# Two-layer mixer and FFN block: attention's stacks on GpSimd's queue, out-projection weights split once, Strassen sums in place

## The chip, the cores and the metric

One core of a Trainium2 chip runs the whole kernel in one launch. The metric is device time in microseconds of an execution. TensorE is the matmul engine (PE), VectorE is DVE, ScalarE is ACT, GpSimd is POOL, SyncE is SP; each has a queue of its own that it works off in order, and a DMA is issued by an instruction in one of these queues.

## What is computed

Two layers over 1024 latent tokens and 256 context tokens, 1024 features, all in float32. Cut to what the change touches (`hc` is the context):

```python
for l in range(DEPTH):                                       # 2
    u_lat = modulate(rms_norm(h, norm1_g[l]), sh1, sc1)
    y_lat, y_ctx = hybrid_mixer(u_lat, u_ctx, ...)           # mLSTM, attention, pool, conv: 256 columns each
    h = h + g1 * (y_lat @ w_out[l])                          # out-projection, 1024 x 1024
    h = h + g2 * swiglu(modulate(rms_norm(h, norm2_g[l]), sh2, sc2), ffn_w_in[l], ffn_w_out[l])
    if l == 0:
        hc = hc + cg1 * (y_ctx @ w_out[l])
        hc = hc + cg2 * swiglu(modulate(rms_norm(hc, ...), ...), ...)

# attention, 4 heads, two softmaxes per head over 1280 keys
s = jnp.einsum('bqhmd,bkhmd->bhmqk', q, k) * (A_HD ** -0.5)  # m = 0, 1; d = 32
p = jax.nn.softmax(s, axis=-1)
o = jnp.einsum('bhqk,bkhe->bqhe', p[:, :, 0] - lam * p[:, :, 1], v)
```

## The kernel before, in words

Activations lie with features on the partitions, eight tiles of 128 features, and tokens along the columns. A float32 product is made of three matmuls on rounded parts: `hi` is a rounded copy (ACT) and `lo` the rest (DVE or POOL subtracts), and `mm3` adds hi x hi, lo x hi and hi x lo. `load_w` (its load is L304, the subtraction L297) loads a raw 128 x 512 weight tile into one of two buffers and splits it into one of five pairs. Calls to the engines pass through a wrapper, so that most instructions have line 165; there tiles tell them apart. The program's text is the order in each engine's queue, apart from what its generators interleave (below); every DMA is issued on SP's queue.

A layer goes through these stages. **Mixers**: projections of the four mixers; `qk_in` makes normalised, rotated q and k, splits them and stores hi and lo to a DRAM scratch (`qks`). **Attention**: `stacks(h)` loads head h's operands from that scratch into 128 partitions. For each m it fills 128 rows of `Qs` with two loads (hi twice, lo twice) and of `Ks` with one (hi and lo, twice), so one plain matmul of 128 rows does the whole product. `dup` makes this source pattern, with an outermost step of 0 that reads everything twice. Head h + 1 is loaded from the third slot of head h. `attention` places its steps in numbered slots of one score group each: scores, maximum (DVE `ls`), exponential (ACT `pr`), the combination of the two softmaxes (POOL and DVE in turn, `combine`), transposes (`atp`), and the product with V (`po`).

**Out-projection**: `out_early` brings in the first six y tiles and four weight tiles during the last head. `out_proj` walks over blocks of tokens (512, 512 and 256 context columns in layer 0; 512, 256 and 256 in layer 1). In each block it loads h, and for each of eight feature tiles `nt` it takes two weight tiles (`out_w`), does 24 matmuls into `ops`, adds the scaled result into h (DVE `h<-ops`), stores h to `hmid`, and advances `later` by three steps. `later` holds the steps of `norm_ffn`'s `chunk` for the blocks done before: squares (ACT `nsq`), their sum over features (PE `nps`), the reciprocal root (DVE), scaling (DVE `h<-h,Af,nrstd`, ACT adds the bias), then the sums of the FFN's Strassen scheme (POOL and DVE into temporary tiles `t`), each split into `Uh` (ACT) and `Ul` (DVE). **FFN**: `ffn_in` loads its weights as `fr`, splits them into `fh` and `fl` (DVE), multiplies into `fps`; then `ffn_out`.

Of the kernel before, what the change touches and what calls it, by code (L numbers as in the profile page):

```python
# [184 lines left out]
class Builder:  # L185
# [299 lines left out]
    def norm_r(self, h, c0, n):  # L485

        nc = self.nc
# [9 lines left out]
        sm = self.T("nsum")[:, :n]  # L497
        self.copy(sm, px[:, :n])
        px = self.PX("nps2")
        nc.tensor.matmul(px[:, :n], self.cb("comb", P), sm, start=True, stop=True)  # L500
        r = self.T("nrstd")[:, :n]
        self.rsqrt(r, px[:, :n], 1e-6, sm)
        return r
# [447 lines left out]
    def qk_in(self, kind, i, c0, n, ps):  # L951
# [24 lines left out]
        for x, v in enumerate((hi, lo)):  # L976
            nc.sync.dma_start(self.qk_scr[kind, 4 * i:4 * i + 4, x, :, c0:c0 + n].bitcast(F32), v.bitcast(F32))
# [179 lines left out]
    def attention(self, early):  # L1157
# [4 lines left out]
        gd = nc.sync.dma_start  # L1162
# [194 lines left out]
    def load_y(self, hi, lo, k, cs):  # L1357

        self.nc.sync.dma_start(lo.bitcast(F32), self.y_scr[k][:, cs])
        self.copy(hi, lo.bitcast(F32))  # L1360
        self.sub_lo(lo, lo.bitcast(F32), hi)

    def first_y(self, k, c0, n):
        t = self.U(f"y{k}", F32R)
        hi, lo = t[:, 0:n], t[:, 512:512 + n]
        self.load_y(hi, lo, k, slice(c0, c0 + n))
        self.y0[k] = (hi, lo)

    def out_w(self, l, nt, pc):
        return self.load_w(self.a["w_out"][l, nt, pc], 512, self.nc.gpsimd, "wo")  # L1370

    def out_early(self, l, chunk):

        self.y0, self.w0 = {}, []
        for i, k in enumerate(self.YORDER[:6]):
            self.first_y(k, *chunk)
            yield
            if i < 4:
                self.w0.append(self.out_w(l, i // 2, i % 2))
                yield  # L1380

    def out_proj(self, l, src, dst, chunks, later):
# [5 lines left out]
        for i, (c0, n) in enumerate(chunks):  # L1388
            v = 1 if c0 < NCTX else 0
            cs = slice(c0, c0 + n)  # L1390
            if i == 0:
                for k in order[6:]:
                    self.first_y(k, c0, n)
                y = self.y0
            else:
                y = {}
                for k in order:
                    y[k] = self.E("yh", KT, F32R)[:, :n], self.E("yl", KT, F32R)[:, :n]
                    self.load_y(*y[k], k, cs)
# [22 lines left out]
    def norm_ffn(self, l, need):  # L1422
# [9 lines left out]
        def chunk(h, c0, n):  # L1432
# [13 lines left out]
            a, b = slice(0, m), slice(m, n)  # L1446
            blk = lambda x: x.rearrange("p (s j) -> p s j", j=P)
            for k in range(4):
                for x in (k, k + 4):
                    hv = h[x][:, :n]  # L1450
                    nc.vector.scalar_tensor_tensor(hv, hv, A[:, x, v:v + 1], r, ALU.mult, ALU.mult)
                    nc.scalar.activation(hv, hv, AF.Identity, bias=B(x))
                yield
# [353 lines left out]
```

## Time and profile before

| What | Value |
|---|---|
| Median of 3 runs | 3509.52 us (3508.51 to 3517.68) |
| Profiled execution | 3513.39 us |
| Its span, first to last instruction | 3511.6 us |
| Mean granted TensorE clock | 0.93 |
| PE busy | 3038.5 us (87%) |
| DVE, ACT, POOL busy | 1950.9, 1356.1, 875.4 us |
| DMA | 368.05 MB, mean 105 GB/s, SP's queue 33.0% of 16 engines |

An engine counts as busy while an instruction of its own runs; DMA issues do not count. "PEclk" or clock is the share of TensorE's full clock that was granted, and a wait is put down to the releaser that came last. Layer 0's attention starts near 554 us and its out-projection lies around 850 to 1012; layer 1's are near 2395 and 2670 to 2816.

### The profile page before, as it was taken

The numbers are of one execution on the slowest core, as the hardware profiler recorded it, in microseconds if no ns is written. First come the engines' busy times: TensorE is split into PE (matmuls) and PEld (weight loads), VectorE is DVE, ScalarE is ACT, GpSimd is POOL, SyncE is SP. The second block draws the span as 40 slices with busy tenths as digits, with TensorE's granted clock in tenths as the row PEclk, the third lists the DMA queues.
The fourth block names the chain that finished last, engine by engine and source line by source line (L and its number), as shares of the span: only waits on it lengthen the run. The fifth ranks groups of instructions, "written<-read, shape, count | busy, mean of one in ns | idle before, by whom it ended". The sixth has DMA issues, their size and how long they took to land. (4 is left out here: it accounts for less than half of the span.)

```text
span 3511.6 us, 44759 instructions
## 1 busy us (share of the span) xinstructions
PE 3038.5 (87%) x16354; PEld 2432.8 (69%) x16354; DVE 1950.9 (56%) x3022; ACT 1356.1 (39%) x2664; POOL 875.4 (25%) x634
## 2 busy tenths in 40 slices
PE   7999883778878999999998898873778779999999
PEld 3757662556667888888886777562557568888787
DVE  5593553874456666663336377543773654544343
ACT  4213442765443222223335422433774543333232
POOL 2241210212533333230001132210232543442000
PEclk9999986898989999999999999986899889999999
DMA  7123221113523443444444311221114422322644
GB/s 264 52 80 98 86 83 57 65 61 107 155 80 108 120 121 99 123 123 155 154 146 156 109 45 43 87 82 56 64 62 128 128 88 81 86 83 60 198 162 138
DMA packets 251246, 368.05 MB, mean 105 GB/s; under 512 B 32401, under 2 KB 109841, under 8 KB 251025
## 3 DMA queue, kind: packets, MB, share of 16 engines
q1 hardware_dynamic: 251024, 365.19, 33.0%
q8 instruction: 129, 2.11, 0.3%
q14 instruction: 93, 0.75, 0.1%
HBM read 295.89 MB, written 69.21 MB: 104 GB/s over the span
## 5 line engine op out<-in xcount | busy, mean ns | idle before, releaser
L165 PE MATMUL fps<-Uh,fh 128*128 128x512 f32 (+1 forms) x1288 | 496.3, 386 | 38.9 <-ACT fh L165 26.1
L165 PE MATMUL fps<-Ul,fh 128*128 128x512 f32 (+1 forms) x1288 | 494.5, 384 | 0.0
L165 PE MATMUL fps<-Uh,fl 128*128 128x512 f32 (+1 forms) x1288 | 493.8, 384 | 0.6 <-DVE fl L165 0.6
L165 ACT ACTIVATE fh<-fr 128x512 fp32r<-128x512 f32 x330 | 207.0, 631 | 529.7 <-PE fps L165 391.0
L165 DVE TENSOR_TENSOR fl<-fr,fh 128x512 fp32r<-128x512 f32 x330 | 270.9, 822 | 133.4 <-ACT fh L165 132.6
L165 PE MATMUL xps<-gl,xh 128*128 128x512 f32 (+1 forms) x880 | 327.3, 373 | 12.8 <-DVE gl L165 12.7
L165 PE MATMUL xps<-gh,xh 128*128 128x512 f32 (+1 forms) x880 | 327.7, 373 | 9.8 <-ACT xh L165 7.5
L165 PE MATMUL xps<-gh,xl 128*128 128x512 f32 (+1 forms) x880 | 326.2, 372 | 0.2 <-DVE xl L165 0.2
L165 PEld LDWEIGHTS fps<-Uh,fh 128*128 128x128 f32 x1288 | 245.6, 191 | 91.5 <-ACT fh L165 28.6
L165 PE MATMUL sc<-Ks,Qs 128*128 128x512 f32 (+1 forms) x400 | 130.5, 437 | 186.6 <-DMA Ks<-qks 108.6
L165 DVE TENSOR_TENSOR ft<-fps,ft 128x512 f32<-128x512 f32 (+1 forms) x230 | 152.7, 664 | 234.9 <-PE fps L165 230.6
L165 PEld LDWEIGHTS fps<-Uh,fl 128*128 128x128 f32 x1288 | 245.2, 190 | 50.3 <-DVE fl L165 1.7
L165 PEld LDWEIGHTS fps<-Ul,fh 128*128 128x128 f32 x1288 | 245.9, 191 | 43.7 <-issue 0.8
L165 DVE TENSOR_REDUCE ls<-sc 128x1 f32<-128x1280 f32 (+1 forms) x144 | 195.4, 1367 | 130.0 <-PE sc L165 129.7
L165 PE MATMUL fmps<-uh,wfh 128*128 128x512 f32 (+1 forms) x592 | 223.8, 378 | 14.9 <-ACT kT L165 14.9
L165 PEld LDWEIGHTS sc<-Ks,Qs 128*128 128x128 f32 x400 | 76.1, 218 | 220.4 <-issue 107.0
L165 ACT ACTIVATE pr<-sc,ls 128x1280 f32<-128x1280 f32 (+1 forms) x144 | 178.4, 1239 | 129.4 <-DVE ls L165 126.1
L165 PE MATMUL fmps<-uh,wfl 128*128 128x512 f32 (+1 forms) x592 | 224.0, 378 | 0.0
L165 PE MATMUL fmps<-ul,wfh 128*128 128x512 f32 (+1 forms) x592 | 223.3, 377 | 0.0
L165 DVE TENSOR_TENSOR gl<-gl,gh 128x512 fp32r<-128x512 f32 (+1 forms) x110 | 70.9, 644 | 264.4 <-ACT gh L165 264.1
L1223 POOL TENSOR_TENSOR pr<-pr,pr 128x1280 f32<-128x1280 f32 (+1 forms) x36 | 95.9, 2663 | 422.7 <-DVE pr L165 225.0
L165 DVE SCALAR_TENSOR_TENSOR acc<-cy,par,acc 128x1286 f32<-128x1286 f32 (+28 forms) x120 | 199.4, 1699 | 1.0
(304 smaller groups left out, 6620.5 us busy)
## 6 DMA issues: line engine op xcount, KB each, us to landing
xr<-in_ffn_out SPq DMA_DIRECT2D x220, 256.0 KB
fr<-in_ffn_in SPq DMA_DIRECT2D x176, 256.0 KB
mw<-in_mod_w SPq DMA_DIRECT2D x160, 256.0 KB
gs<-ft SPq DMA_DIRECT2D x99, 256.0 KB
wor<-in_w_out SPq DMA_DIRECT2D x96, 256.0 KB
gl<-gs SPq DMA_DIRECT2D x88, 256.0 KB
wfr<-in_w_fm SPq DMA_DIRECT2D x56, 256.0 KB
Ks<-qks SPq DMA_DIRECT2D x16, 640.0 KB
```

Source lines behind the costliest of these rows:

```text
L165: ins = f(*args, **kw)
L1223: nc.gpsimd.tensor_tensor(pr[0][:, :n], pr[0][:, :n], pr[1][:, :n], ALU.add)
```

## The change

- The 44 stores of `qk_in` and the 48 loads of Q and K stacks (32 and 16) are issued on POOL's queue; the loads of V stay on SP's.
- `out_w` splits each of the 16 out-projection weight tiles in a layer's first block only, and stores hi and lo to a DRAM scratch (`wos`, 256 KB each); later blocks load hi and lo from there. In counts over both layers: raw loads 96 before and 32 now, `wos` stores 64, `wos` loads 96.
- In layer 1 the blocks are 512 and 512, as in the FFN, not 512, 256 and 256.
- The squares of the norm are summed inside the out-projection, one `nt` behind the result (`norm_sums`, `norm_fin`); the context block's are not formed there.
- The Strassen sums overwrite h's tiles, in the order in which the FFN uses them (B11, B22, T2, T3, T1, B21, T4). Per 512 columns DVE does 8 scalings, 20 splits and 12 differences of 256 columns, POOL 4 differences and 8 splits; the temporaries are gone.
- `out_early` first issues the six y loads, with each split three steps behind, and then the four weight tiles.

```diff
+    def norm_sums(self, n):
         px = self.PX("nps")
         for k in range(KT):
+            v = yield
             sq = self.T("nsq")
-            v = h[k][:, c0:c0 + n]
-            nc.scalar.activation(sq[:, :n], v, AF.Square)
+            self.nc.scalar.activation(sq[:, :n], v[:, :n], AF.Square)
             g = slice((k % 4) * 32, (k % 4) * 32 + 32)
-            nc.tensor.matmul(px[g, :n], self.cb("one", 32), sq[:, :n], start=(k < 4), stop=(k >= 4))
+            self.nc.tensor.matmul(px[g, :n], self.cb("one", 32), sq[:, :n], start=(k < 4), stop=(k >= 4))
...
-            nc.sync.dma_start(self.qk_scr[kind, 4 * i:4 * i + 4, x, :, c0:c0 + n].bitcast(F32), v.bitcast(F32))
+            nc.gpsimd.dma_start(self.qk_scr[kind, 4 * i:4 * i + 4, x, :, c0:c0 + n].bitcast(F32), v.bitcast(F32))
...
-        gd = nc.sync.dma_start
+        gd = nc.gpsimd.dma_start
...
+    def out_w(self, l, nt, pc, first):
+
+        if first:
+            w = self.load_w(self.a["w_out"][l, nt, pc], 512, self.nc.gpsimd, "wo")
+            for x in range(2):
+                self.nc.sync.dma_start(self.wo_scr[nt, pc, x], w[x][:, :512].bitcast(F32))
+            return w
+        w = [self.wp.tile([P, 544], F32R, tag=t, name=t, bufs=5) for t in ("wh", "wl")]
+        for x in range(2):
+            self.nc.sync.dma_start(w[x][:, :512].bitcast(F32), self.wo_scr[nt, pc, x])
+        return w
...
+        for i in range(len(ks) + 3):
+            if i < len(ks):
+                self.load_y(ks[i], *chunk, True)
+            if i >= 3:
+                self.split_y(ks[i - 3])
             yield
-            if i < 4:
-                self.w0.append(self.out_w(l, i // 2, i % 2))
-                yield
+        for i in range(4):
+            self.w0.append(self.out_w(l, i // 2, i % 2, True))
+            yield
...
+            squares = self.norm_sum(n) if not v else None
...
-                w = [self.w0.pop(0) if self.w0 else self.out_w(l, nt, pc) for pc in range(2)]
+                w = [self.w0.pop(0) if self.w0 else self.out_w(l, nt, pc, i == 0) for pc in range(2)]
...
+                if squares and nt:
+                    squares.send(h[nt - 1])
             if i == 0:
                 self.ux.close()
-            todo = itertools.chain(todo, later(h, c0, n))
+            if squares:
+                squares.send(h[KT - 1])
+                todo = itertools.chain(todo, later(h, c0, n))
...
-            if v:
-                return
-            r = yield from self.norm_r(h, 0, n)
-            B = lambda k: mod[:, 24 + k, v:v + 1]
...
+            for k in (0, 4, 1, 5, 2, 6, 3, 7):
+                hv = h[k][:, :n]
+                nc.vector.scalar_tensor_tensor(hv, hv, A[:, k, v:v + 1], r, ALU.mult, ALU.mult)
+                nc.scalar.activation(hv, hv, AF.Identity, bias=mod[:, 24 + k, v:v + 1])
+                if k >= 4:
+                    yield
...
+            def split(i, src, eng):
+                for k in range(4):
+                    hi, lo = (x[:, i, cs].rearrange("p (s j) -> p s j", j=P) for x in state["U"][k])
+                    self.copy(hi, half(*src(k)))
+                    eng(lo, half(*src(k)), hi.bitcast(F32), ALU.subtract)
+                    if k % 2:
+                        yield
+            def minus(a, b, eng):
+                for k in range(4):
+                    eng(half(*b(k)), half(*a(k)), half(*b(k)), ALU.subtract)
+            u1a, u1b, u2a, u2b = ((lambda k, x=x, i=i: (h[k + x], i)) for x in (0, 4) for i in range(2))
+            yield from split(self.B11, u1a, d)
+            minus(u1b, u1a, g)
+            minus(u2b, u1b, d)
+            yield from split(self.B22, u2b, g)
             for k in range(4):
+                d(half(*u2b(k)), half(*u2b(k)), half(*u1a(k)), ALU.subtract)
+            yield from split(self.T2, u2b, d)
+            yield from split(self.T3, u1b, d)
+            yield from split(self.T1, u1a, g)
+            yield from split(self.B21, u2a, d)
+            for k in range(4):
+                d(half(*u2a(k)), half(*u2a(k)), half(*u2b(k)), ALU.subtract)
+            yield from split(self.T4, u2a, d)
...
-            oc = LATE if need else ((256, 512), (768, 256), (1024, 256))
...
-            self.out_proj(l, src, mid, oc, norm)
+            self.out_proj(l, src, mid, ch, norm)
```

How this moves instructions is shown at three places. The first is POOL's queue at the start of layer 1's attention, before and then with the change (`czl` belongs to the convolution, `pr` is a combine, `qks` the scratch of q and k):

```order
L297 TENSOR_TENSOR czl<-acc_16513,czh 128x512
L297 TENSOR_TENSOR czl<-acc_16514,czh 128x512
L1223 TENSOR_TENSOR pr_19540<-pr_19540,pr_19541 128x1280
L1223 TENSOR_TENSOR pr_19602<-pr_19602,pr_19603 128x1280
L1223 TENSOR_TENSOR pr_19681<-pr_19681,pr_19682 128x1280
L1223 TENSOR_TENSOR pr_19751<-pr_19751,pr_19752 128x1280
```

```order
L297 TENSOR_TENSOR czl<-acc_16514,czh 128x512
L297 TENSOR_TENSOR czl<-acc_16515,czh 128x512
L1190 DMA Qs_19528<-qks_16202 64x1x1024 x2
L1192 DMA Ks_19531<-qks_16202 128x1x1280
L1190 DMA Qs_19533<-qks_16202 64x1x1024 x2
L1192 DMA Ks_19536<-qks_16202 128x1x1280
L1190 DMA Qs_19565<-qks_16202 64x1x1024 x2
L1192 DMA Ks_19568<-qks_16202 128x1x1280
L1190 DMA Qs_19570<-qks_16202 64x1x1024 x2
L1192 DMA Ks_19573<-qks_16202 128x1x1280
L1237 TENSOR_TENSOR pr_19541<-pr_19541,pr_19542 128x1280
```

Twelve loads, those of two heads, now stand in POOL's queue ahead of its first combine; later, six stand between two combines at each head.

The second is SP's queue in the first out-projection block of layer 1, before and then with the change (`wor` raw weights, `wos` the scratch of split ones, `yl` the next block's y, `hmid` the result):

```order
L1402 DMA h<-hscr 128x512 x8
L1412 DMA hmid_21338<-h 128x512
L304 DMA wor<-in_w_out 128x512 x2
L1359 DMA yl<-ys_16203 128x256 x2
L1412 DMA hmid_21338<-h 128x512
L1359 DMA yl<-ys_16203 128x256 x2
L304 DMA wor<-in_w_out 128x512 x2
L1359 DMA yl<-ys_16203 128x256 x4
L1412 DMA hmid_21338<-h 128x512
L304 DMA wor<-in_w_out 128x512 x2
```

```order
L1430 DMA h<-hscr 128x512 x8
L1440 DMA hmid_21348<-h 128x512
L1390 DMA wos_20802<-woh 128x512
L1390 DMA wos_20802<-wol 128x512
L1390 DMA wos_20802<-woh 128x512
L1390 DMA wos_20802<-wol 128x512
L1440 DMA hmid_21348<-h 128x512
L304 DMA wor<-in_w_out 128x512 x2
L1383 DMA yl<-ys_16204 128x512 x2
L1390 DMA wos_20802<-woh 128x512
L1390 DMA wos_20802<-wol 128x512
```

Between two results there are now four stores of split weights, and the next raw weight loads stand behind them; a store of `wol` can go only when POOL has made it.

The third is DVE's queue where layer 1's out-projection gives way to the FFN, before and then with the change (`Ul` is the low part of a Strassen sum, `fl` that of an FFN weight):

```order
L165 SCALAR_TENSOR_TENSOR h<-h,Af_21339,nrstd 128x256
L165 TENSOR_TENSOR Ul_21758<-h,Uh_21757 128x128
L165 TENSOR_TENSOR t_22709<-h 128x128
L165 TENSOR_TENSOR Ul_21758<-h,Uh_21757 128x2x128
L165 TENSOR_TENSOR Ul_21758<-t_22708,Uh_21757 128x2x128
L165 TENSOR_TENSOR Ul_21758<-t_22709,Uh_21757 128x2x128
L165 TENSOR_TENSOR fl<-fr,fh 128x512 x5
L165 TENSOR_TENSOR ft<-fps,ft 128x256
```

```order
L165 TENSOR_TENSOR Ul_21816<-h,Uh_21815 128x256
L165 TENSOR_TENSOR h<-h 128x2x128 x4
L165 TENSOR_TENSOR Ul_21810<-h,Uh_21809 128x256
L165 TENSOR_TENSOR Ul_21812<-h,Uh_21811 128x256
L165 TENSOR_TENSOR Ul_21814<-h,Uh_21813 128x256
L165 TENSOR_TENSOR Ul_21816<-h,Uh_21815 128x256
L165 TENSOR_TENSOR fl<-fr,fh 128x512 x5
L165 TENSOR_TENSOR ft<-fps,ft 128x256
```

Before, the last rows split all seven sums of one of the four feature tiles of a 256 block; now they are the last sum, T4, of all four tiles of a 512 block. In both the FFN's first weight splits come behind them.

## Rows read from the trace of the kernel before

**Rows 1.** Page section 2: TensorE's busy tenths in 40 equal slices of the span.
```profile
PE   7999883778878999999998898873778779999999
```

**Rows 2.** Windows: length, busy time (instructions) of PE, PEld, DVE, ACT, POOL, clock, DMA share, GB/s.
```profile
2400.00:2446.00 46.00, 1.41 (x3) 0.83 (x3) 3.78 (x5) 4.97 (x8) 0.00 (x0) 0.51 0.16 59
...
2493.00:2541.00 48.00, 35.02 (x293) 26.73 (x293) 35.52 (x42) 35.12 (x67) 11.63 (x4) 0.93 0.15 58
...
870.00:880.00 10.00, 10.00 (x45) 8.11 (x44) 4.47 (x7) 6.19 (x11) 5.21 (x4) 1.00 0.84 261
...
2734.00:2842.00 108.00, 62.16 (x336) 48.80 (x334) 68.46 (x114) 55.43 (x128) 58.49 (x62) 0.78 0.37 115
```

**Rows 3.** Tile Ks: idle time of the scores' engine before them, us and times, by releaser.
```profile
  DMA Ks<-qks: 108.6, 9
```

**Rows 4.** Timeline of SP's queue (start us, us, form) where attention starts, both layers.
```profile
554.42 1.14 SPq L1176 DMA_DIRECT2D Qs<-qks  x2
...
2394.98 0.57 SPq L1176 DMA_DIRECT2D Qs<-qks  x1
...
2401.20 11.38 SPq L1176 DMA_DIRECT2D Qs<-qks  x2
```

**Rows 5.** Timeline of PE, scores of layer 1, idle before and releaser in brackets.
```profile
2422.79 1.41 PE L165 MATMUL sc<-Ks,Qs 128*128 128x512 f32 x3 [25.26 <-DMA Ks<-qks]
2446.11 2.47 PE L165 MATMUL sc<-Ks,Qs 128*128 128x512 f32 x6 [21.91 <-DMA Ks<-qks]
...
2492.55 1.41 PE L165 MATMUL sc<-Ks,Qs 128*128 128x512 f32 x3 [5.29 <-DMA Ks<-qks]
...
2496.80 0.83 PE L165 MATMUL sc<-Ks,Qs 128*128 128x512 f32 x3
...
2540.61 1.41 PE L165 MATMUL sc<-Ks,Qs 128*128 128x512 f32 x3 [6.71 <-DMA Ks<-qks]
...
2588.88 1.41 PE L165 MATMUL sc<-Ks,Qs 128*128 128x512 f32 x3 [5.37 <-DMA Ks<-qks]
```

**Rows 6.** Timeline of PE, layer 0, attention's start and third head.
```profile
572.43 0.66 PE L165 MATMUL pt<-cst,hs 128*128 128x128 f32 x2 [11.23 <-DVE hs L165]
...
611.12 2.48 PE L165 MATMUL sc<-Ks,Qs 128*128 128x512 f32 x6 [24.86 <-DMA Ks<-qks]
...
715.23 1.41 PE L165 MATMUL sc<-Ks,Qs 128*128 128x512 f32 x3 [3.81 <-DMA Ks<-qks]
```

**Rows 7.** Timeline of DVE: the out-projection's results, layer 0 and then layer 1.
```profile
858.56 0.75 DVE L165 SCALAR_TENSOR_TENSOR h<-ops,mod,h 128x512 f32<-128x512 f32 x1 [6.50 <-PE ops L165]
...
897.47 0.75 DVE L165 SCALAR_TENSOR_TENSOR h<-ops,mod,h 128x512 f32<-128x512 f32 x1 [4.82 <-PE ops L165]
...
1011.97 0.48 DVE L165 SCALAR_TENSOR_TENSOR h<-ops,mod,h 128x256 f32<-128x256 f32 x1 [1.11 <-PE ops L165]
...
2716.17 0.75 DVE L165 SCALAR_TENSOR_TENSOR h<-ops,mod,h 128x512 f32<-128x512 f32 x1 [4.82 <-PE ops L165]
...
2815.84 0.48 DVE L165 SCALAR_TENSOR_TENSOR h<-ops,mod,h 128x256 f32<-128x256 f32 x1 [4.57 <-PE ops L165]
```

**Rows 8.** Groups of instructions: count, busy us, mean ns, idle before and releasers.
```profile
L297 POOL TENSOR_TENSOR wol<-wor,woh 128x512 fp32r<-128x512 f32 x96 | 131.0, 1372 | 184.8 <-ACT woh L165 183.2 <-PE ops L165 1.1
...
L165 ACT ACTIVATE woh<-wor 128x512 fp32r<-128x512 f32 x96 | 59.6, 625 | 87.2 <-DMA wor<-in_w_out 62.5 <-PE ops L165 16.1 <-issue 8.6
```

**Rows 9.** Timeline of POOL: two combines of attention, layer 1.
```profile
2453.03 2.90 POOL L1223 TENSOR_TENSOR pr<-pr,pr 128x1280 f32<-128x1280 f32 x1 [73.03 <-DVE pr L165]
...
2510.86 2.90 POOL L1223 TENSOR_TENSOR pr<-pr,pr 128x1280 f32<-128x1280 f32 x1 [7.31 <-PE atp L165]
```

**Rows 10.** Timeline of PE: the FFN of layer 1 gets going.
```profile
2842.18 0.58 PE L165 MATMUL fps<-Uh,fl 128*128 128x256 f32 x1 [0.32 <-DVE fl L165]
```

**Rows 11.** Timeline of DVE: scalings and one split, layer 1.
```profile
2732.12 4.14 DVE L165 SCALAR_TENSOR_TENSOR h<-h,Af,nrstd 128x512 f32<-128x512 f32 x4
...
2747.87 0.41 DVE L165 TENSOR_TENSOR Ul<-h,Uh 128x256 fp32r<-128x256 f32 x1
```

More of the change, by code (lines that the diff above doesn't have):

```diff
@@ L482, in mod_vec, with norm_sum, norm_fin, norm_r @@
             yield
-    def norm_r(self, h, c0, n):
-        nc = self.nc
+    def norm_sum(self, n):
+        gen = self.norm_sums(n)
+        next(gen)
+        return gen
+    def norm_sums(self, n):
         px = self.PX("nps")
         for k in range(KT):
+            v = yield
             sq = self.T("nsq")
-            v = h[k][:, c0:c0 + n]
-            nc.scalar.activation(sq[:, :n], v, AF.Square)
+            self.nc.scalar.activation(sq[:, :n], v[:, :n], AF.Square)
             g = slice((k % 4) * 32, (k % 4) * 32 + 32)
-            nc.tensor.matmul(px[g, :n], self.cb("one", 32), sq[:, :n], start=(k < 4), stop=(k >= 4))
+            self.nc.tensor.matmul(px[g, :n], self.cb("one", 32), sq[:, :n], start=(k < 4), stop=(k >= 4))
+        self.nsum = self.T("nsum")[:, :n]
+        self.copy(self.nsum, px[:, :n])
+        yield
+    def norm_fin(self, n):
+        px = self.PX("nps2")
+        self.nc.tensor.matmul(px[:, :n], self.cb("comb", P), self.nsum, start=True, stop=True)
+        r = self.T("nrstd")[:, :n]
+        self.rsqrt(r, px[:, :n], 1e-6, self.nsum)
+        return r
+    def norm_r(self, h, c0, n):
+        sums = self.norm_sum(n)
+        for k in range(KT):
+            sums.send(h[k][:, c0:c0 + n])
             if k == KT // 2 - 1:
                 yield
[L497 to L503, printed above, removed]
+        return self.norm_fin(n)
     def finish(self, gen):
@@ L1355, with split_y, load_y @@
     YORDER = (0, 1, 4, 5, 6, 7, 2, 3)
-    def load_y(self, hi, lo, k, cs):
-        self.nc.sync.dma_start(lo.bitcast(F32), self.y_scr[k][:, cs])
+    def split_y(self, k):
+        hi, lo = self.y[k]
         self.copy(hi, lo.bitcast(F32))
         self.sub_lo(lo, lo.bitcast(F32), hi)
[L1363 to L1370, printed above, removed]
-    def out_early(self, l, chunk):
-        self.y0, self.w0 = {}, []
-        for i, k in enumerate(self.YORDER[:6]):
-            self.first_y(k, *chunk)
+    def load_y(self, k, c0, n, first):
+        if first:
+            t = self.U(f"y{k}", F32R)
+            self.y[k] = t[:, 0:n], t[:, 512:512 + n]
+        else:
+            self.y[k] = self.E("yh", KT, F32R)[:, :n], self.E("yl", KT, F32R)[:, :n]
+        self.nc.sync.dma_start(self.y[k][1].bitcast(F32), self.y_scr[k][:, c0:c0 + n])
+    def out_w(self, l, nt, pc, first):
+        if first:
+            w = self.load_w(self.a["w_out"][l, nt, pc], 512, self.nc.gpsimd, "wo")
[6 more added lines that the diff above has]
+        return w
+    def out_early(self, l, chunk):
+        self.y, self.w0 = {}, []
+        self.wo_scr = self.dp.tile([KT, 2, 2, P, 512], F32, name=f"wos{l}")
+        ks = self.YORDER[:6]
+        for i in range(len(ks) + 3):
[3 more added lines that the diff above has]
+                self.split_y(ks[i - 3])
             yield
-            if i < 4:
-                self.w0.append(self.out_w(l, i // 2, i % 2))
-                yield
+        for i in range(4):
+            self.w0.append(self.out_w(l, i // 2, i % 2, True))
+            yield
     def out_proj(self, l, src, dst, chunks, later):
@@ L1390, in out_proj @@
             cs = slice(c0, c0 + n)
[L1391 to L1399, printed above, removed]
+            if i:
+                self.y = {}
+            for k in order[0 if i else 6:]:
+                self.load_y(k, c0, n, i == 0)
+                self.split_y(k)
+            y = self.y
             h = [self.E("h", 9) for _ in range(KT)]
+            squares = self.norm_sum(n) if not v else None
             for k in range(KT):
@@ L1690, in run @@
                 self.vgw = self.tm_w(self.vg_w(l), 272, nc.gpsimd)
-            self.mixers(l, u, later, self.out_early(l, oc[0]))
+            self.mixers(l, u, later, self.out_early(l, ch[0]))
             self.mx.close()
```

29 lines of the change are left out of this document (4 added, 25 removed).

## The prediction

> **What bounds the kernel now.** I read the page's slices first, then the windows where TensorE is thin, then who was waited for there. TensorE is busy eight or nine tenths nearly everywhere [rows 1]; the FFN and the projections are bounded by its matmuls, and a change that leaves those alone can only win in the holes. Two of the holes are where this change works.
>
> The first is the start of attention in each layer. For 46 us of layer 1 TensorE does 1.41 us of work, DVE 3.78, ACT 4.97, POOL nothing, while the DMA engines are 0.16 busy at 59 GB/s [rows 2]: nobody works. By tile, the scores waited 108.6 us in 9 waits for the stack of K [rows 3]. SP issues the first Q load at 554.42 in layer 0 and 2394.98 in layer 1, right as the last projection frees the buffers, and is then held 11.38 us in the issue of two Q loads [rows 4]: the queue takes nothing more. TensorE, idle from 2422.79 − 25.26 = 2397.5, makes one score at 2422.79 and the next at 2446.11 [rows 5]; in layer 0 it goes on at 611.12 [rows 6]. A head's stacks in layer 1 are 4 x 256 + 2 x 640 = 2304 KB and its period 48 us, which is 49 GB/s: the later heads too run at the pace of the loads, with a wait of 5.29, 6.71 and 5.37 us at each head's start [rows 5], and 3.81 at layer 0's third [rows 6]. A share of 0.15 is 2.4 of 16 engines, and in the out-projection the same SP queue moves 261 GB/s at 0.84 [rows 2]. So these loads do not lack bandwidth; each sits on a few engines. The Trainium skill, DMA: Bandwidth & Descriptors, section "Why a DMA increments its semaphore by 16 and not by 1", says a transfer is dealt to the largest number up to 16 that divides both patterns' outermost sizes; the stacks read their source twice, so that size is 2. The trace agrees with its 2.4 engines.
>
> The second is the out-projection. With the weights there in time, a 128-row result of 512 columns takes (897.47 − 858.56) / 7 = 5.56 us of matmul, 44.5 us a block [rows 7]. The two later blocks of layer 1 hold the same 512 columns yet take 2815.84 − 2716.17 = 99.7 us, and those of layer 0, 512 + 256 columns, 114.5 us for 66.7 of matmul [rows 7]. In layer 1 TensorE is 62.16 of 108 us busy there, DVE 68.46, POOL 58.49 [rows 2]: each weight tile is copied by ACT (625 ns) and subtracted by POOL (1372 ns) again in every block [rows 8], in queues that they share with the norm's and the Strassen work.
>
> **The change, part by part.** The sum is made against the profiled execution, 3513.4 us; its median is 3.9 lower. A measurement of this kernel tells about 0.3% from no change.
>
> *Stacks and q/k stores on POOL's queue* (48 loads, 44 stores). Where does a load on this queue take its engines from? The trace has no transfer on it. At the slow end nothing changes, 0 us. At the fast end a head moves at the 261 GB/s of [rows 2]: 2304 KB in 8.8 us, 2560 KB (layer 0) in 9.8. I take the fast end, since the row nearest to it is of the same chip and core with 14 engines idle. Layer 1: buffers free at 2397.5, 8.8 us of transfer and some 2 of landing give the second score at 2408 instead of 2446.1: −38. Layer 0: the same from about 557, plus what has to land for the step before (at 572.43, itself 11.23 us late [rows 6] because its small load lies in the same queue) gives 573 instead of 611.1: −38. Heads 2 to 4 of layer 1: the waits are 17.4 us; the score after each comes about 4.1 us later (2496.80 − 2492.55 [rows 5]) instead of 2.5, so 1.6 x 3 more; 0.8 of each wait would be there anyway: −20. Layer 0's heads are longer by a unit of the context's; the third waits 3.81 and the fourth is taken for like it, by the same count: −8. POOL pays an issue per load. In layer 1 its first combine comes after 73 us of idleness [rows 9], so the twelve loads ahead of it are covered. Each later head has six between two combines that lie some 10 us apart and take 2.9 [rows 9]; I charge 4 us for both layers. Sum 38 + 20 + 38 + 8 − 4 = 100 less, between ends of 0 and about −110.
>
> *Split weights kept in DRAM.* It takes 64 ACT copies and 64 POOL subtractions (64 x 0.625 = 40 us, 64 x 1.372 = 88 us [rows 8]) out of the later blocks, and adds 64 stores and 96 loads of 256 KB for 64 loads less, 25 MB net. The first block of each layer pays: 12 raw weight loads (4 come early), 32 stores, and 8 tiles each of y, h in and h out, near 17 MB inside 44.5 us. By 261 GB/s at 0.84 the engines' full rate would be 310, so 17 MB need 55 us: +10 a layer, 0 at best; +20 if SP's order holds raw loads behind stores that wait for POOL. Together +20.
>
> *Later blocks.* With POOL and ACT relieved, layer 1's one block of 512 should run at 44.5 plus some 7 where evacuations stand behind sums on DVE: 52 instead of 99.7, −48. Two blocks of 256 cost the same columns, so the merge itself takes no matmul time; it spares 16 weight tiles. In layer 0, 44.5 + 30 (the 256 block needs 8.4 MB of weights, 27 us at 310, more than its 22.2 of matmul) + 15 for the queue of sums: 90 instead of 114.5, −24. Ends: 0 and −80 together.
>
> *Norm and sums.* Squares inside the loop ride on ACT beside matmuls: nothing while ACT has room (55.43 of 108 [rows 2]). In place and in order of use changes when the FFN can begin. In layer 1 it starts in earnest at 2842.18, 26.3 us after the last result at 2815.84 [rows 7, 10]. Now a whole 512 block is left then: about 3 us of root, 8 scalings (4.14 us for 4 [rows 11]), 20 splits and 12 differences of 256 columns at 0.41 [rows 11], 24.5 us of DVE, and the FFN's own splits stand behind them all; with the chain's hops 34: +8. Layer 0 ends on the context block, which covers that: 0.
>
> Sum of the out-projection: 20 − 48 − 24 + 8 = −44. All: −144; 3513.4 − 144 = 3369.4, at the median 3365.5: **3366 us**.
>
> **Rivals.**
> *A: POOL's queue deals the stacks to the same few engines.* For it: the access pattern is unchanged, and with it what was slow; against it: the engines are idle and the queue is another. Only the −44 is left: 3466. The section of the Trainium skill named above has it that SP's queue takes the lowest-numbered engines while POOL's moves on by a cursor, or takes 16. By that the six loads of a head spread over at least 12 engines, the longest, 640 KB, at the present 58 GB/s of one pair in 11.3 us instead of a head in 8.8, and the sum would be 5 us smaller at most; no row here shows it.
> *B: POOL issues late because DVE holds it off.* DVE is busy 35.52 of 48 us a head [rows 2]. If an issue of 1 us only advances in DVE's pauses (26%), six take 23 us between combines 10 us apart; less the 7.5 us of three slots by which weights are due, some 6 us at each of six boundaries: 36, 3402. For it: the trace shows no issue of POOL's, so nothing excludes it; against it: the first heads, most of the gain, find DVE idle (3.78 of 46). The Trainium skill, SBUF — State Buffer, section "Who interferes with whom", has such a rule: some DVE operations lock POOL out of the port through which it writes descriptors. No row here bears it out yet.
> *D: the out-projection becomes bound by transfers or SP.* SP now meets, ahead of each raw load, four stores that wait for POOL. If that loop runs at 8 us a result instead of 5.56, each first block costs 20, and the weights of the later blocks come late too: no gain in total, 3410. For it: 17 MB against 310 GB/s. Against: two weight tiles are loaded ahead.
> *C, slower: an issue costs POOL much more.* Six loads of c each stand ahead of a combine that has 7.1 us of room and 7.5 of slack; at six boundaries 6c − 14.6, and 6c − 12 at two starts: 48c − 112. It eats the whole −144 from c = 5.3 us. At 6 us it is 176 and 3542. For it: POOL has never issued here; against: SP's ordinary issue is 1.14 for two [rows 4].
>
> **The numbers.** Forecast 0.50, A 0.15, B 0.15, D 0.15, C 0.05. The range 3325 to 3440: below, first blocks at no cost (−20), no issue cost (−4), transition unchanged (−8) and the later blocks at their floor (−8); above, B and D together (3446) nearly; A and C are left out, 0.2. Faster by over 0.3%: all but C and half-failures, 0.93; same 0.02; slower 0.05.
>
> **What will show it.** A queue of POOL's in the page's list of queues with the stacks; no TensorE wait for the stack of K over 2 us past the first; second scores near 573 and 2408 less what came before; scores 2.5 us apart across heads. Combines late by DVE's or the issue's doing (B, C) would show as ACT's transposed weights waiting for POOL. First block of the out-projection 55 us, layer 1's second 52, FFN start 34 after the last result. I am wrong if K still lands at 48 to 60 GB/s, or if results of the first block come 8 us apart.

## The result, and the profile after

The changed kernel takes 3410.97 us (median of 4 runs, 3400.94 to 3415.06) against 3509.02 before, a ratio of 0.9711 with a 95% interval of 0.9685 to 0.9738. Faster was forecast, at 3366 and within 3325 to 3440; 144 us were to go, about 100 went. The profiled execution has a span of 3413.3 us, 98.3 less than before. Cut at the same instructions in both traces, the 98.3 us lie as follows (us; the forecast is that of the prediction's sum):

| Stretch | Before | After | Change | Forecast |
|---|---|---|---|---|
| Layer 0, start to the convolution's last variance | 559.2 | 552.3 | −6.9 | 0 |
| Layer 0, from there to the second score | 51.9 | 31.3 | −20.6 | −38 |
| Layer 0, rest of attention | 220.3 | 214.9 | −5.4 | −8 |
| Layer 0, first out-projection block | 66.1 | 75.8 | +9.7 | +10 |
| Layer 0, later blocks | 114.5 | 110.4 | −4.1 | −24 |
| FFN of layer 0 and mixers of layer 1 | 1385.3 | 1361.3 | −24.0 | 0 |
| Layer 1, last projection to second score | 48.9 | 32.4 | −16.5 | −38 |
| Layer 1, rest of attention | 195.3 | 177.7 | −17.6 | −20 |
| Layer 1, first block | 74.8 | 83.3 | +8.5 | +10 |
| Layer 1, later block(s) | 99.7 | 62.4 | −37.3 | −48 |
| Layer 1, last result to first FFN product | 19.5 | 33.6 | +14.1 | +8 |
| Rest | 676.2 | 677.9 | +1.7 | 0 |

(The prediction also charged 4 us of POOL issue to attention.) So, by the prediction's terms, the first blocks and the later heads came near, attention's starts and the later blocks were priced too high and the FFN's start too low, and 31 us came from where nothing was forecast.

**Attention's start.** The page's list of queues (packets, MB, share of 16 engines) has a new row for the changed kernel, POOL's queue:

```profile
q0 software_dynamic: 43968, 30.07, 4.7%
```

By tile, what the engine of the scores waited for by K's loads (us, times), and these loads' time from issue to landing:

```profile
  DMA Ks<-qks: 57.6, 4
...
DMA to landing us min/median/max: 15.5/24.2/31.4
```

The wait for K went from 108.6 us in 9 [rows 3] to 57.6 in 4: it is gone at the later heads and has shrunk at the first ones. Two windows at the first heads (length, busy time of PE, PEld, DVE, ACT, POOL, clock, DMA share, GB/s) show what is left:

```profile
560.00:581.00 21.00, 0.00 (x0) 0.00 (x0) 0.00 (x0) 0.00 (x0) 1.43 (x2) 0.50 1.00 161
2358.00:2377.00 19.00, 0.98 (x2) 0.83 (x3) 0.00 (x0) 0.00 (x0) 1.48 (x3) 0.50 0.84 136
```

Nobody computes, as in [rows 2], but now the DMA engines are 1.00 busy where they were 0.16, at 161 GB/s where there were 59. The forecast's fast end had 261. The stage before attention ends in layer 0 with the convolution's last variance (`cvar`), before and then with the change:

```profile
559.21 1.98 PE L165 MATMUL cvar<-csq,cst 128*128 128x512 f32 x4 [2.22 <-ACT csq L165]
```

```profile
552.33 1.98 PE L165 MATMUL cvar<-csq,cst 128*128 128x512 f32 x4 [1.29 <-ACT csq L165]
```

The scores on PE (start, duration, idle before and its releaser), layer 0, layer 1, where the idle time begins at the last projection, and the start of layer 1's third head:

```profile
581.22 1.41 PE L165 MATMUL sc<-Ks,Qs 128*128 128x512 f32 x3 [25.88 <-DMA Ks<-qks]
583.67 1.41 PE L165 MATMUL sc<-Ks,Qs 128*128 128x512 f32 x3 [1.05 <-DMA Ks<-qks]
...
2376.02 1.41 PE L165 MATMUL sc<-Ks,Qs 128*128 128x512 f32 x3 [29.73 <-DMA Ks<-qks]
2378.40 1.41 PE L165 MATMUL sc<-Ks,Qs 128*128 128x512 f32 x3 [0.97 <-DMA Ks<-qks]
...
2461.30 0.84 PE L165 MATMUL sc<-Ks,Qs 128*128 128x512 f32 x3 [0.78 <-ACT pr L165]
```

Against [rows 5, 6] the second scores stand 31.3 and 32.4 us behind the stage before, not 51.9 and 48.9; at the third head, where 6.71 us were waited for K, there is no such wait. POOL's own timeline at layer 1's start and at one later head:

```profile
2344.01 1.36 POOL L1190 DMA_DIRECT2D Qs<-qks  x2 [16.84 <-PE tmps L165]
...
2376.17 0.65 POOL L1190 DMA_DIRECT2D Qs<-qks  x1 [16.13 <-DMA Qs<-qks]
...
2460.05 2.91 POOL L1237 TENSOR_TENSOR pr<-pr,pr 128x1280 f32<-128x1280 f32 x1 [7.03 <-PE atp L165]
2462.89 1.34 POOL L1190 DMA_DIRECT2D Qs<-qks  x2
2464.20 0.81 POOL L1192 DMA_DIRECT2D Ks<-qks  x1
```

An issue takes POOL 0.65 to 0.84 us, beside a busy DVE too; six of them fit between two combines. The 16.13 us of idleness are an issue's wait for an earlier load; what stands behind it are loads and the first combine, and that waited for DVE in the end.

**Out-projection.** DVE's results, layer 0's first block, its last result, and then layer 1 (answering to [rows 7]):

```profile
825.61 0.75 DVE L165 SCALAR_TENSOR_TENSOR h<-ops,mod,h 128x512 f32<-128x512 f32 x1 [6.40 <-PE ops L165]
...
874.27 0.75 DVE L165 SCALAR_TENSOR_TENSOR h<-ops,mod,h 128x512 f32<-128x512 f32 x1 [2.46 <-PE ops L165]
...
984.66 0.48 DVE L165 SCALAR_TENSOR_TENSOR h<-ops,mod,h 128x256 f32<-128x256 f32 x1 [2.73 <-PE ops L165]
...
2591.04 0.75 DVE L165 SCALAR_TENSOR_TENSOR h<-ops,mod,h 128x512 f32<-128x512 f32 x1 [5.71 <-PE ops L165]
...
2639.36 0.75 DVE L165 SCALAR_TENSOR_TENSOR h<-ops,mod,h 128x512 f32<-128x512 f32 x1 [2.91 <-PE ops L165]
...
2648.64 0.74 DVE L165 SCALAR_TENSOR_TENSOR h<-ops,mod,h 128x512 f32<-128x512 f32 x1
...
2669.80 0.74 DVE L165 SCALAR_TENSOR_TENSOR h<-ops,mod,h 128x512 f32<-128x512 f32 x1
...
2701.79 0.75 DVE L165 SCALAR_TENSOR_TENSOR h<-ops,mod,h 128x512 f32<-128x512 f32 x1 [5.99 <-PE ops L165]
```

And the FFN's first product of layer 1 on PE before; then, with the change, the first product and the one that answers to [rows 10], and DVE's first split of an FFN weight:

```profile
2835.38 0.58 PE L165 MATMUL fps<-Uh,fh 128*128 128x256 f32 x1 [16.76 <-ACT fh L165]
```

```profile
2735.39 0.58 PE L165 MATMUL fps<-Uh,fh 128*128 128x256 f32 x1 [29.27 <-ACT fh L165]
...
2741.83 0.58 PE L165 MATMUL fps<-Uh,fl 128*128 128x256 f32 x1 [0.32 <-DVE fl L165]
```

```profile
2735.37 0.69 DVE L165 TENSOR_TENSOR fl<-fr,fh 128x512 fp32r<-128x512 f32 x1 [4.69 <-DMA fr<-in_ffn_in]
```

The product of [rows 10] now stands 40.0 us behind the last result, not 26.3. DVE is through with the sums 28.9 us after the last result; the other 4.69 us are a wait for a load of an FFN weight in this one execution. In six of the runs below that have the same sums (e3, e4, e4b, e5, e6, e8) the first product stands at 30.7 us, not 33.6.

In layer 1 the first block's results come 6.9 us apart on average (48.3 / 7) where there were 5.56; then there are 21.2 us between the first and the second result of the second block (22.4 before).

### The profile page after: what moved, and what is told of

Same layout as the page of the kernel before. It is cut to its first block, busy times and chain, and to the rows that moved or that the text cites. A ratio compares the mean times of both kernels' runs of the same rounds, so it can differ in the third digit from the quotient of the medians.

```text
span 3413.3 us, 44185 instructions
## 1 busy us (share of the span) xinstructions
PE 3020.0 (88%) x16144; PEld 2399.7 (70%) x16144; DVE 1935.9 (57%) x3023; ACT 1318.5 (39%) x2605; POOL 846.8 (25%) x650
## 5 line engine op out<-in xcount | busy, mean ns | idle before, releaser
L165 PEld LDWEIGHTS xps<-gl,xh 128*128 128x128 f32 x880 | 168.5, 192 | 41.4 <-DVE gl L165 13.3
```

The lines of the kernel that those rows point to most:

```text
L165: ins = f(*args, **kw)
```

## The experiments

All are compared with the kernel before on their own chip. Ratios with 95% intervals; the changed kernel is at 0.9711 [0.9685, 0.9738].

| Run | Ratio | Interval |
|---|---|---|
| e1 stacks alone | 0.9819 | 0.9799 to 0.9839 |
| e2 stores alone | 0.9932 | 0.9910 to 0.9954 |
| e3 change, stacks back on SP | 0.9904 | 0.9880 to 0.9927 |
| e5 change, stacks in pieces on SP | 0.9615 | 0.9595 to 0.9634 |
| e4 change, second head later (did not move) | 0.9710 | 0.9687 to 0.9732 |
| e4b change, second head behind a combine | 0.9681 | 0.9666 to 0.9696 |
| e6 change, weights split in each block | 0.9727 | 0.9705 to 0.9750 |
| e7 change, sums as before | 0.9668 | 0.9649 to 0.9686 |
| e8 change, scratch stored by POOL | 0.9710 | 0.9694 to 0.9727 |
| e12 change, squares after the block | 0.9685 | 0.9670 to 0.9699 |
| e10 = e5 + e7 | 0.9572 | 0.9557 to 0.9586 |
| e13 = e5 + e7 + e12 | 0.9530 | 0.9508 to 0.9552 |

The intervals of e4, e4b, e6, e7, e8 and e12 overlap that of the changed kernel. The gains of e7 and e12 come again in e10 against e5 and in e13 against e10, where the intervals stand apart; that of e4b rests on its trace.

**The two halves of the move to POOL's queue.** In the kernel before, one line each:

```diff
 e1 -        gd = nc.sync.dma_start
    +        gd = nc.gpsimd.dma_start
 e2 -            nc.sync.dma_start(self.qk_scr[kind, 4 * i:4 * i + 4, x, :, c0:c0 + n].bitcast(F32), v.bitcast(F32))
    +            nc.gpsimd.dma_start(self.qk_scr[kind, 4 * i:4 * i + 4, x, :, c0:c0 + n].bitcast(F32), v.bitcast(F32))
 e3 (in the changed kernel) the line of e1 undone
```

> The kernel before with the 48 stack loads alone on POOL's queue. Theory 1 (the loads spread over all engines, and that is worth 37 us at the two first heads and 23 at the later ones): 3509 - 60 = 3449, second scores 32 us after the last projection instead of 49 and 52. Rival (the stacks gain only together with the q/k stores, because one queue then holds both the store and the load): within 10 us of 3509.

> The kernel before with the 44 q/k stores alone on POOL's queue. Theory 1 (SP's queue no longer holds the rope tables and the mLSTM reloads behind stores that wait): the mixers of layer 1 shorter by 18 and of layer 0 by 7, 3509 - 25 = 3484. Rival (the gain in the mixers comes from the other parts, or the stores ask too much of POOL): 3509 or more.

> The changed kernel with the stack loads back on SP's queue and nothing else. Theory 1 (the two halves add up): 3411 + 60 = 3471, K waits of some 25 us at the first heads and 4 to 7 at later ones. Rival (what the stacks gained hangs on SP's queue being full of stores): under 3430.

Measured, of some 3510 us: e1 −64, e2 −24, and e3 67 above the changed kernel (0.9904 against 0.9711). All three went as theory 1 had it, and the two halves add. What the change does beside them is then e3 less e2: −34 + 24 = −10 us for the whole out-projection part, and since the intervals of the two overlap (0.9880 to 0.9927 and 0.9910 to 0.9954), these 10 us can't be told from zero. In e1 the second scores stand 31.9 and 31.3 us behind the stage before, as in the changed kernel. In e2 the mixers of layer 1, from the first to the last product of the feature projections, take 287.1 us; before 305.4, changed kernel 287.7. Why the stores count is in the waits of layer 1's mixers (us in total, times, longest), before and then with the change:

```profile
POOL gq L970 <- DMA ropec<-in_rope: 32.1, 5, 9.9
DVE hs L165 <- DMA so<-os: 18.5, 4, 5.1
DVE ropes L165 <- DMA ropes<-in_rope: 17.9, 4, 6.7
```

```profile
POOL gq L984 <- DMA ropec<-in_rope: 14.8, 2, 9.1
DVE ropes L165 <- DMA ropes<-in_rope: 9.1, 3, 5.1
```

The loads of the mLSTM's gate (`so`) and of the rope tables stood in SP's queue behind q/k stores, of which every second one (lo) waits for POOL's subtraction. With the stores elsewhere, the wait for `so` is gone and the other two are halved; in e2, with the stores alone moved, it is gone too and they are 14.5 and 9.9.

**The shape of the stack loads.** e5 puts the stacks back on SP, with no repeated source:

```diff
-        gd = nc.gpsimd.dma_start
+        gd = nc.sync.dma_start
-                for x in range(2):
-                    gd(Qm[x * 64:x * 64 + 64, q0:NT].bitcast(F32), dup(self.qk_scr[0, mp, x, :, q0:NT].bitcast(F32)))
+                for x in range(4):
+                    gd(Qm[x * 32:x * 32 + 32, q0:NT].bitcast(F32), self.qk_scr[0, mp, x // 2, :, q0:NT].bitcast(F32))
...
+                for x in range(2):
+                    gd(Km[x * 64:x * 64 + 64, 0:NT].bitcast(F32),
+                       self.qk_scr[1, mp].rearrange("a r n -> (a r) n").bitcast(F32))
```

> The changed kernel with the stacks on SP's queue, but each duplicate as a load of its own (32 rows of Q, 64 of K, no repeated source), 96 loads instead of 48. Theory 1 (the outermost size of 2 is what kept a load on two engines): a head moves at 230 GB/s or more, second scores 18 us after the last projection, 3411 - 25 = 3386. Rival A (SP's queue itself is the limit, whatever the shape): 3471, like the stacks put back. Rival B (bandwidth of small rows is the limit as on POOL's queue): 3411.

Measured 0.9615, 34 us below the changed kernel. K lands 6.6 us after issue (median), and the window 561 to 566 us in layer 0, columns as above, has this:

```profile
DMA to landing us min/median/max: 3.9/6.6/8.6
```

```profile
561.00:566.00 5.00, 1.23 (x3) 0.62 (x3) 3.66 (x5) 2.12 (x4) 0.00 (x0) 0.50 1.02 238
```

238 GB/s at 1.02, on the queue and the engines that had 59 at 0.16 with the repeated source. So it was the access pattern, not SP's queue, that kept a load on 2.4 engines; rival A of this run is out. The second score, which [rows 6] had at 611.12:

```profile
566.21 2.47 PE L165 MATMUL sc<-Ks,Qs 128*128 128x512 f32 x6 [3.98 <-DMA Ks<-qks]
```

It stands 14.8 us behind the stage before (551.4) instead of 51.9.

Why POOL's queue reaches only 161 GB/s with all engines busy is not in the size of its packets. The packets of the whole run, before and in e1, whose one edit moves the stacks:

```profile
DMA packets 251246, 368.05 MB, mean 105 GB/s; under 512 B 32401, under 2 KB 109841, under 8 KB 251025
```

```profile
DMA packets 280590, 368.18 MB, mean 107 GB/s; under 512 B 61744, under 2 KB 139184, under 8 KB 280368
...
q0 software_dynamic: 33536, 20.04, 3.1%
```

The move adds 29344 packets and 29343 packets under 512 B, with 0.13 MB between them, so the 20 MB of the stacks themselves go in as many large packets as before. The mean on POOL's queue is 0.6 KB (20.04 MB in 33536 packets); the "600-byte packets" of the expectations below are this mean, and no packet's size. What differs is the engines that a load holds. Windows with SP's queue before (layer 1's start), then with POOL's and the six loads of layer 1's fourth head, issued from 2462.89 on (columns as above):

```profile
2403.00:2422.00 19.00, 0.00 (x0) 0.00 (x0) 0.00 (x0) 0.00 (x0) 0.00 (x0) 0.50 0.13 52
```

```profile
2469.00:2473.00 4.00, 3.11 (x31) 2.27 (x27) 3.74 (x6) 3.43 (x8) 1.44 (x1) 1.00 0.76 169
2484.00:2487.00 3.00, 2.99 (x22) 2.02 (x20) 2.48 (x6) 3.00 (x7) 1.90 (x1) 1.00 0.25 102
```

On SP's queue all the loads together hold 0.13, two engines of 16. On POOL's the six hold 0.76, twelve, and near their end 0.25, four. That reads as two engines a load on either queue: SP's puts every load on the same two, POOL's lays the loads side by side. The twelve loads of two heads then fill the 16 and move no more, 161 GB/s against 169. By these shares a busy engine moves some 25 GB/s where two or four work, 14 where twelve do, 10 where sixteen do, and 15 in e5's pieces; why it slows down, no run here shows.

**Who shares the engines at the first head.**

```diff
 e4  -            if k % (4 * len(nblk)) == 2 and k // (4 * len(nblk)) < 3:
     +            if k % (4 * len(nblk)) == (7 if k < 4 * len(nblk) else 2) and k // (4 * len(nblk)) < 3:
 e4b  the same with 5, and each load of head 1 ordered behind POOL's first combine:
     +                    if h == 1:
     +                        self.after(ins, self.first)
     ...
```

> The changed kernel with the second head's stacks issued in slot 7 of the first head, not slot 2. Theory 1 (at the first head all 16 DMA engines are busy with 600-byte packets, so the second head's loads delay the first's by about 10 us in each layer): 3411 - 20 = 3391, first K wait 16 us instead of 26 and 30. Rival (each load is slow by itself, not the engines full): 3411 within 5, or more if the second head is then late.

e4 measured 0.9710, no change, but it says nothing: the program's text does not set the order in POOL's queue alone, and the loads stayed where they were, all but one K (timeline of POOL, layer 0):

```profile
594.82 2.90 POOL L1237 TENSOR_TENSOR pr<-pr,pr 128x1280 f32<-128x1280 f32 x1 [10.86 <-DVE pr L165]
597.67 0.82 POOL L1192 DMA_DIRECT2D Ks<-qks  x1
```

> The changed kernel with the second head's stacks ordered behind the first combine on POOL (an order on one queue, no new wait), which the run before this one was meant to do and did not. Theory 1 (16 engines full of 600-byte packets, shared by two heads): a head alone needs 2560 KB at 160 GB/s, 16 us, so the second scores come 22 us after the last projection instead of 31 and 32, 3411 - 18 = 3393. Rival (a load on this queue is slow by itself): second scores unchanged, 3411, or up to 3425 if the second head is then late.

e4b measured 0.9681, some 10 us better, not 18, but the second scores moved as expected: 24.1 and 21.8 us behind the stage before instead of 31.3 and 32.4. The second head's loads do delay the first's. But a head alone still needs its 20 us and more,

```profile
DMA to landing us min/median/max: 20.0/23.5/26.3
```

at a DMA share that falls from 0.77 to 0.51 in the last 20 us before the scores, as loads on two engines each come to their end. So sharing is one half of what was left, and loads on too few engines the other.

**The out-projection's first block.** It took the 9 to 10 us more that were forecast, for another reason. TensorE's busy time in layer 1's first block, of all instructions and then of the sums of squares (`nps`) alone (columns as above; the second view has no POOL):

```profile
2591.00:2639.40 48.40, 47.74 (x183) 31.44 (x181) 11.76 (x16) 14.66 (x25) 13.66 (x11) 1.00 0.81 280
```

```profile
2591.00:2639.40 48.40, 7.32 (x14) 0.96 (x14) 0.00 (x0) 0.00 (x0) 1.00 0.81 280
```

TensorE is 47.74 of 48.40 us busy; 7.32 are the sums of squares that the change moved into the block. Three runs look at it.

```diff
 e6  -                w = [self.w0.pop(0) if self.w0 else self.out_w(l, nt, pc, i == 0) for pc in range(2)]
     +                w = [self.w0.pop(0) if self.w0 else self.out_w(l, nt, pc, True) for pc in range(2)]
     ...
     -            for x in range(2):
     -                self.nc.sync.dma_start(self.wo_scr[nt, pc, x], w[x][:, :512].bitcast(F32))
 e8  -                self.nc.sync.dma_start(self.wo_scr[nt, pc, x], w[x][:, :512].bitcast(F32))
     +                self.nc.gpsimd.dma_start(self.wo_scr[nt, pc, x], w[x][:, :512].bitcast(F32))
 e12 -            squares = self.norm_sum(n) if not v else None
     ...
     -                if squares and nt:
     -                    squares.send(h[nt - 1])
     ...
     -            r = self.norm_fin(n)
     +            r = yield from self.norm_r(h, 0, n)
```

> The changed kernel without the scratch of split weights: every block loads raw tiles and splits them, as before. Theory 1 (the scratch costs 9 us in each first block and gives back more in the later ones): first blocks 44 us from first to last result's spacing instead of 54, later blocks 30 to 40 us longer in sum over both layers, 3411 + 15 = 3426. Rival (what the later blocks gained comes from the merge and the sums, not from the scratch): 3411 - 18 = 3393.

> The changed kernel with the 64 stores of split weights issued on POOL's queue. Theory 1 (first blocks are slow because the raw loads stand on SP behind stores that wait for POOL): results of the first block 5.6 us apart instead of 7, 3411 - 18 = 3393. Rival (the DMA engines are full in the first block): 3411 within 5.

> The changed kernel with the norm's squares formed after a block, as before, not inside it. Theory 1 (the first block is bound by TensorE, which spends 7.3 of its 48.4 us on the sums of squares): first block's results 5.6 to 6 us apart instead of 6.9, about 6 us less in each first block, given back in part where the next block or the FFN waits for the root: 3411 - 6 = 3405, within 10. Rival (the first block is bound by its 17 MB): first block unchanged at 48.4 us, later parts 5 to 10 longer, 3418.

e6, with no stores at all, and e8, with the stores on POOL, have the same first block in layer 1, 45.9 us from first to last result, against 48.3 (DVE's results in e8, then its window, columns as above):

```profile
2594.31 0.75 DVE L165 SCALAR_TENSOR_TENSOR h<-ops,mod,h 128x512 f32<-128x512 f32 x1 [7.08 <-PE ops L165]
...
2640.17 0.75 DVE L165 SCALAR_TENSOR_TENSOR h<-ops,mod,h 128x512 f32<-128x512 f32 x1 [5.97 <-PE ops L165]
```

```profile
2594.00:2641.00 47.00, 47.00 (x184) 31.90 (x182) 13.63 (x16) 15.16 (x25) 25.13 (x33) 1.00 0.90 316
```

So beside the squares the stores in SP's order cost 2.4 us a block; theory 1 of e8, 5.6 us a result, is out as long as the squares are there, and "17 MB" is out as what held the block at 48.3: e8 moves as many bytes in less time, at 316 GB/s. e8's total doesn't move; its later blocks are no shorter (64.2 us in layer 1 against 62.4). e6 loses in the later blocks (119.3 and 63.6 us against 110.4 and 62.4); in sum 0.9727, 6 us worse, which the intervals don't separate from the changed kernel: the scratch pays, if at all, in layer 0, whose third block has half the columns for the same weights. In layer 1 it is not the scratch that brought 99.7 us down to 62.4, since 63.6 stand without it; nor, by the runs below, the new order of the sums (55.6 with the old one) or the place of the squares (57.2). What each of these leaves is the merge into one block of 512; no run undoes that alone.

e12's results of layer 1's first block:

```profile
2582.18 0.75 DVE L165 SCALAR_TENSOR_TENSOR h<-ops,mod,h 128x512 f32<-128x512 f32 x1 [5.66 <-PE ops L165]
...
2598.83 0.75 DVE L165 SCALAR_TENSOR_TENSOR h<-ops,mod,h 128x512 f32<-128x512 f32 x1 [2.24 <-PE ops L165]
...
2606.25 0.75 DVE L165 SCALAR_TENSOR_TENSOR h<-ops,mod,h 128x512 f32<-128x512 f32 x1 [1.87 <-PE ops L165]
...
2628.89 0.75 DVE L165 SCALAR_TENSOR_TENSOR h<-ops,mod,h 128x512 f32<-128x512 f32 x1 [2.91 <-PE ops L165]
```

Up to the fourth they come 5.55 us apart, so the squares did set the pace; from then on 7.4, and the block ends only 1.6 us sooner. That this is the order of the stores is argued, not shown; what speaks for it is e8, which with the same bytes but the stores elsewhere has 6.7 there, squares and all. The larger gain lies behind the first block: later blocks 100.7 and 57.2 us instead of 110.4 and 62.4. In all 0.9685, some 9 us.

**The order of the sums.** e7 puts `chunk`'s loop over feature tiles back (scale tiles k and k + 4, four sums into temporaries, four splits, all low parts on DVE), with the squares as the change has them:

```diff
-            yield from split(self.B11, u1a, d)
...
-            yield from split(self.T4, u2a, d)
+            for k in range(4):
...
+                t, z = self.T("t12"), self.T("t34")
...
+                    self.copy(hi, src)
+                    nc.vector.tensor_tensor(lo, src, hi.bitcast(F32), ALU.subtract)
```

> The changed kernel with the Strassen sums of the kernel before (feature tile by feature tile, with temporaries, all low parts on DVE). Theory 1 (in order of use, all nine h buffers stay held until the last sum, so the next block's h and the FFN's weights load late): the 21 us between first and second result of the second block shrink to 8, FFN start 26 to 30 us after the last result instead of 40, 3411 - 25 = 3386. Rival (order of use and POOL's share of the splits are what made the later blocks shorter): 3411 + 15 = 3426.

Measured 0.9668, 15 us better than the changed kernel. The first two results of layer 1's second block:

```profile
2640.01 0.74 DVE L165 SCALAR_TENSOR_TENSOR h<-ops,mod,h 128x512 f32<-128x512 f32 x1
2647.87 0.74 DVE L165 SCALAR_TENSOR_TENSOR h<-ops,mod,h 128x512 f32<-128x512 f32 x1
```

7.9 us between them where the change has 21.2; the 22.4 before, with the same sums, say that their order alone does not make it short. One reason stands in SP's timeline: the loads of the second block's h, in the changed kernel and then in e7.

```profile
2665.01 2.92 SPq L1430 DMA_DIRECT2D h<-hscr  x4
```

```profile
2643.90 0.32 SPq L1430 DMA_DIRECT2D h<-hscr  x1
```

There are nine h buffers for eight tiles. Tile by tile, the first come free early, and h is reloaded from 2643.90 on, one after the other; in order of use every tile is read up to the last sums, and the next four are issued at 2665.01. DVE's queue has been ordered to match, the second result behind nearly all sums, so that buffer and order can't be told apart here. More buffers weren't tried. The later blocks take 98.2 and 55.6 us (changed kernel 110.4 and 62.4), and the FFN begins 29.0 us after the last result instead of 33.6, or of the 30.7 of the six runs named above.

**Together.**

> The stacks in pieces on SP's queue together with the Strassen sums of the kernel before. Theory 1 (attention's start and the later blocks are separate stretches of the path, so the gains add): 35 and 15 below the changed kernel, 3411 - 50 = 3361. Rival (the sums' gain overlaps with the loads'): 3380, as the pieces alone.

> The stacks in pieces on SP's queue, the Strassen sums of the kernel before and the norm's squares after the block: all three gains of the single runs (35, 15 and 9 us below the changed kernel). Theory 1 (they lie in separate stretches): 3366 - 9 = 3357. Rival (with the sums tile by tile the squares in the block were no longer in the way, since it was the order of sums that held up DVE): 3366 within 4.

e10 measured 3365.71 us, e13 3353.02 (3344.47 to 3355.62): 165 us less than before and 63 less than the changed kernel, so the gains add (the last is 15 us where 9 were expected, which the intervals allow). e13 keeps of the change the q/k stores on POOL, the scratch and the blocks of 512.

## Why the prediction was right and wrong

- **Attention bound by the stack loads, on few engines: right.** e1 takes 64 us away with one line, and e5 shows that the shape of the source is what counts. The Trainium skill, DMA: Bandwidth & Descriptors, section "Rules for kernel authors", has it that a leading repetition of c copies keeps a load on at most c engines. The runs agree: on SP's queue 238 GB/s at 1.02 without one (e5) against 59 at 0.16 with it, and on POOL's six such loads held 0.76 and their end 0.25, which reads as two engines each.
- **"At the fast end a head moves at the 261 GB/s ... I take the fast end": wrong in size.** The step that priced 2 x 38 gave 20.6 + 16.5. It took the rate of loads that use all engines for loads that still held two each: one head moved some 160 to 170 GB/s on twelve engines, its last loads 102 on four, and at the start two heads shared the 16. Taking the sharing away gave 17.8 us (e4b), taking the repetition away, on SP's queue, 36 (e5, from 31.3 and 32.4 us to 14.8 and 13.0). Later heads, −28 forecast, gave −23.
- **q/k stores at no cost or gain: wrong.** They were counted among POOL's issues only; that SP's queue was moved past other loads was not priced. It was worth 24 us (e2), and makes up for most of the 39 that the first heads fell short. Without it the time would have been about 3435, at the upper end of the stated range; that the total came so near is in part luck.
- **First blocks +20: right in sum (+18.2), wrong in cause.** Not 17 MB: e8 moved as many bytes faster. Two things hold the block at nearly the same length. One is TensorE, by 7.3 us of squares that the prediction called free "while ACT has room"; it looked at ACT and not at the matmul behind each square. The other, as far as e8 shows it, is the order of the stores, which the prediction had only as its worse end. Without the stores the block takes 45.9 us (e6, e8), without the squares 46.7 (e12), and 38.9 before, with neither; both out at once wasn't tried.
- **Later blocks −72: −41.4.** "Some 7 where evacuations stand behind sums" and "15 for the queue of sums" were too small: the order of the sums, taken as harmless here, costs 19 us in both layers (e7), and the squares another 15 (e12). "With POOL and ACT relieved" was not the reason in layer 1: e6 takes that relief back and loses 1.2 us there.
- **FFN start +8: +14.1.** DVE's 24.5 us were right in kind and measured 28.9; 4.69 more are the late weight load of the profiled execution. In the six runs without that wait it is +11.2, of which e7 takes 1.7 back.
- **Rivals.** A, the same few engines for all loads, did not occur (share 1.00, not 0.16). What the prediction set beside it, six loads on at least 12 engines, is what the 0.76 shows; but it let a pair keep its 58 GB/s, and with twelve engines at work a pair moved about 28, so the 5 us that it took off were too few. B and C: an issue takes 0.65 to 0.84 us with DVE busy as with DVE idle, far from the 5.3 us from which C decides, and the lockout that the Trainium skill, SBUF — State Buffer, section "Who interferes with whom", speaks of shows in no row. D, "no gain in total" from the out-projection, was nearer than the forecast: the −44 came out at −9 by the table, −10 by e3 less e2. Its loop of stores is there, as far as argued above, with results 7.4 us apart from the fourth on once the squares are out (e12), near its 8; beside the squares it costs 2.4 us a block (e8).
- **Small sums.** 2304 KB at 261 GB/s are 9.0 us, not 8.8, and by the count given layer 0's two later heads are 9, not 8. Neither changes a reading.

## What to carry to other kernels

Look at the outermost dimension of a load that lands slowly while the DMA engines are idle: an extra issue per copy is cheaper than a pattern that repeats its source. When a transfer leaves a queue, price what stood behind it there, and when a reduction moves into a loop, price it on the engine that bounds the loop, here TensorE and not ACT. Work in order of the tiles, which frees their buffers early, can be worth more than work in the order in which its results are used. And a mean size of packets can be the size of none: look at how many are small.

## What was not expected of the hardware

Stack loads with a repeated source held two engines between them on SP's queue (share 0.13, 52 GB/s) and two each on POOL's, six loads twelve (0.76, 169 GB/s). Twelve loads filled the 16 engines (1.00) and moved no more, 161 GB/s, against 238 at 1.02 of pieces without repetition. Moving them to POOL's queue added 29343 packets under 512 B and 0.13 MB to the same 20 MB. A load of K took a median of 24.2 us to land on POOL's queue, 23.5 when the second head's loads came later (e4b), and 6.6 in pieces.
